# A two-layer hybrid backbone: small attention rows loaded first, output weights split during the convolution, and the value products of differential attention in parts

## The chip, the cores and the metric

The kernel runs on one core of one Trainium2 chip. The core has a matrix engine (PE, whose weight loads are listed apart as PEld), three engines for elementwise work (DVE, ACT, POOL), a queue engine (SP) that issues most DMAs, and 16 DMA engines that carry the transfers. The metric is the device time of one execution in microseconds. Three runs of the kernel before took 3598.65, 3591.5 and 3580.62 us, so their median is 3591.5 us.

## The reference

A backbone of two layers works on 1024 latent tokens and 256 context tokens, 1024 wide. Layer 0 mixes by gated linear attention and grouped-query attention, layer 1 by a Hyena convolution (512 channels) and differential attention (4 heads). Each mixer ends in one output projection, and a squared-ReLU MLP follows. The part that the change touches is the mixer of layer 1:

```python
def diff_attend(q, keys, vals, lam):
    ...
        s = jnp.einsum('bqhcd,bshcd->bhcqs', qblk, keys).astype(jnp.float32) * hd ** -0.5
        pr = jax.nn.softmax(s, axis=-1)
        a = (pr[:, :, 0] - lam * pr[:, :, 1]).astype(vals.dtype)
        return jnp.einsum('bhqs,bshv->bqhv', a, vals)
...
    y = out(diff_attend(q, jnp.concatenate([kc, k], axis=1), jnp.concatenate([vc, v], axis=1), lam))
...
    y = jnp.concatenate([y_c, y_d], axis=-1) @ w_out
```

Each head has two score matrices (c = 0, 1), whose softmaxes are subtracted with a learned factor lam before one product with 128-wide values. The result is normalised and scaled by a learned row `diff_g`. The Hyena half (`y_c`) is a projection, a short convolution, and two long convolutions by Fourier transform, each gated.

## The kernel before

**Numbers and tiles.** All matrices are float32. Most products are done as three faster products of parts: `split` (L92) copies a tile to a high part of type fp32r on ACT and subtracts it from the source on DVE (or POOL) for a low part, and `mm3` (L98) multiplies high by high, high by low and low by high into one PSUM bank. A PSUM bank holds 128 x 512 floats. The token axis is cut into NT = 10 tiles of 128 (two of context, eight of latent tokens).

**Order.** The program is written as generators. `weave` runs several of them side by side, each at a rate given in the code (a yield is one step), and `pipelined` keeps several items in flight. A scheduler then fixes the order of each engine's instructions when the program is built. Every engine runs its own list in that order, so an instruction that waits holds up all those behind it on its engine. SP issues DMAs in order too, and a DMA's issue can wait for a buffer.

**Layer 1, in time order** (times of the profiled execution):

- Up to about 2175 us the projection of layer 1 makes q, k and v of the differential attention. `in_proj1_v` (L1639) copies v to DRAM (`dv`) tile by tile, and q and k go to DRAM (`dq`, `dk`) from `qk_hi` and `qk_lo` (L1763), in parts.
- From there `diff_attn` (L2168) and `hyena` (L2503) are woven. The Hyena part begins with `hy_columns` (L1690): 12 blocks of 128 columns, 0 to 11; the weights of blocks 0 to 3 are loaded ahead, during the projection. A block loads its weights (`cb_raw`, two buffers, by SP), splits them (`cb_hi` on ACT, `cb_lo` on POOL, two buffers each), multiplies (`hc_ps`, L1683 to L1685), convolves (`hy_cv` on ACT and DVE), transposes (`cv_ps`) and stores (`hv<-hy_st`, issued by ACT, one buffer).
- `diff_attn` loads its keys and queries with `load` (L2175: `dkT`, two DMAs a head, and the buffer of the values `dvT`) and `load_q` (L2186: `dqT`, two DMAs for a group of 512 queries). Its work is 8 units, 4 heads by 2 query groups. A unit has 10 key steps. Each of the first eight key steps does one of the eight score rows of the next unit (`s_ps`, three pieces each, eviction by DVE maxima and ACT exponentials), then for its own unit `front` (four 128 x 128 transposes of probabilities into `pt_ps`, the one PSUM bank with the tag `tr`, and a copy `pt` by ACT) and `back` (one float32 product into `o_ps` with the values). 26 steps of the weave lie between the start of `diff_attn` and its first score.
- The load of the learned row, `df_gain` (L2263), of the lambda vectors, `df_lp`, and the small arithmetic on them (L2265 to L2276, on DVE and ACT) stand in the code after the first `load` and `load_q` and ahead of those 26 steps.
- After the last block and `diff_attn`, `hy_conv` (L1962) does the Fourier convolutions of the Hyena half: `forward`, `spectrum`, `backward`. The rest of the weave is `proj_half` (L1097), the attention half of the output projection (`ho_ps`, at rate 0.27). At the end `wo_rest` (L1089) loads and splits the four weight tiles for the Hyena half (`wo_raw`, `wo_hi` on ACT, `wo_lo` on POOL), `mlp_in` (L2339) reads the convolution's result back (`y_in<-hy`) and finishes the projection (`op_ps`), and the MLP follows.

## Time and profile before

| what | value |
|---|---|
| median of three runs | 3591.5 us (3580.62 to 3598.65) |
| the profiled execution's own time | 3587.32 us |
| its span in the profile | 3585.5 us |
| mean granted PE clock | 0.941 |
| PE busy in the span | 3158.2 us, 88% |
| DVE / ACT / POOL busy | 77% / 44% / 32% |
| all DMA traffic | 516.36 MB, mean 144 GB/s |

The profile shows one execution, and engines are busy side by side, so the shares don't add up to one. In the views, a row of a timeline has its start, its length, the engine, the source line, and what was written from what. In square brackets is the idle time ahead of it and the work that ended it. The stretch that the change touches begins at about 1970 us (the value projection) and ends at about 2890 us (the last output projections of layer 1). The rest of the span is the same code before and after.

### The profile page before, as it was taken

The page shows a single profiled execution, that of the slowest core. Times are in us where ns is not written, and L with a number is a line of the kernel's source. Part 1 is how long each engine was busy: PE and PEld are TensorE (multiplying, and loading weights), DVE is VectorE, ACT ScalarE, POOL GpSimd, SP SyncE. Part 2 cuts the span into 40 slices and gives each one's busy share as a digit, 9 for nine tenths or more (in the row PEclk, how much of TensorE's full clock was granted, in tenths as well). Part 3 has the DMA queues.
Part 4 walks back from the last instruction along what each step waited for, and adds up shares of the span by engine and source line. Part 5 has one row for each costly group of instructions (what it writes and reads, how often), then busy time and mean ns, then how long its engine had stood idle before and what let it go on. Part 6 is the DMA issues. An engine that isn't in the chain of part 4 may idle for free. (4 is left out here: it accounts for less than half of the span.)

```text
span 3585.5 us, 42317 instructions
## 1 busy us (share of the span) xinstructions
PE 3158.2 (88%) x13936; PEld 2451.6 (68%) x13936; DVE 2747.6 (77%) x4482; ACT 1560.3 (44%) x3186; POOL 1134.4 (32%) x796
## 2 busy tenths in 40 slices
PE   8888899799988999989998994988848689998996
PEld 4766677577766888767786773666636567887885
DVE  6788988787578666789888771767787589877989
ACT  5444666455563222343334631566632352225433
POOL 0254655323231222355554120100010212215654
PEclk9989999899999999999999997999979899999998
DMA  6543111667652333554543642222445635437442
GB/s 216 158 138 116 43 46 47 183 201 239 229 179 100 129 131 117 186 167 151 169 151 106 193 146 91 73 87 70 130 125 176 206 127 183 148 134 271 150 150 100
DMA packets 315961, 516.36 MB, mean 144 GB/s; under 512 B 39282, under 2 KB 138610, under 8 KB 315613
## 3 DMA queue, kind: packets, MB, share of 16 engines
q1 hardware_dynamic: 264708, 430.86, 36.9%
q10 hardware_dynamic: 41816, 49.24, 4.0%
q0 software_dynamic: 9216, 33.56, 3.4%
q8 instruction: 110, 1.80, 0.2%
q14 instruction: 111, 0.90, 0.1%
HBM read 364.21 MB, written 149.35 MB: 143 GB/s over the span
## 5 line engine op out<-in xcount | busy, mean ns | idle before, releaser
L95 POOL TENSOR_TENSOR dn_w_lo<-dn_b,dn_w_hi 128x512 fp32r<-128x512 f32 x224 | 358.8, 1626 | 317.3 <-ACT dn_w_hi L94 311.6
L1533 PE MATMUL dn_ps<-dn_w_hi,dn_h_hi 128*128 128x512 f32 x896 | 360.9, 403 | 40.5 <-DVE accy L1515 7.0
L1535 PE MATMUL dn_ps<-dn_w_hi,dn_h_lo 128*128 128x512 f32 x896 | 358.1, 400 | 13.4 <-DVE dn_h_lo L95 13.3
L1534 PE MATMUL dn_ps<-dn_w_lo,dn_h_hi 128*128 128x512 f32 x896 | 358.5, 400 | 9.4 <-POOL dn_w_lo L95 9.3
L95 POOL TENSOR_TENSOR w_lo<-up_w,w_hi 128x512 fp32r<-128x512 f32 x106 | 146.3, 1390 | 567.4 <-ACT w_hi L94 539.7
L94 ACT ACTIVATE dn_h_hi<-dn_h 128x512 fp32r<-128x512 f32 x224 | 139.1, 625 | 267.8 <-PE dn_ps L1534 172.3
L95 DVE TENSOR_TENSOR dn_h_lo<-dn_h,dn_h_hi 128x512 fp32r<-128x512 f32 x224 | 231.4, 1051 | 22.6 <-ACT dn_h_hi L94 20.3
L1533 PEld LDWEIGHTS dn_ps<-dn_w_hi,dn_h_hi 128*128 128x128 f32 x896 | 173.3, 193 | 87.7 <-DVE accz L1515 9.7
L765 POOL TENSOR_TENSOR gq_acc<-gq_acc,gq_p 128x512 f32<-128x512 f32 x128 | 183.8, 1436 | 88.5 <-ACT gq_p L754 85.1
L261 DVE SCALAR_TENSOR_TENSOR ada_acc<-w_ada,sc,ada_acc 128x512 f32<-128x512 f32 x224 | 194.2, 899 | 21.0 <-DMA w_ada<-in_w_ada 20.2
L1535 PEld LDWEIGHTS dn_ps<-dn_w_hi,dn_h_lo 128*128 128x128 f32 x896 | 173.4, 193 | 53.3 <-DVE dn_h_lo L95 16.7
L1534 PEld LDWEIGHTS dn_ps<-dn_w_lo,dn_h_hi 128*128 128x128 f32 x896 | 173.3, 193 | 48.9 <-POOL dn_w_lo L95 13.2
L95 DVE TENSOR_TENSOR gq_lo<-gq_p,gq_hi 128x512 fp32r<-128x512 f32 x168 | 176.2, 1061 | 19.7 <-ACT gq_hi L94 17.5
L94 ACT ACTIVATE s_hi<-up_w 128x512 fp32r<-128x512 f32 x128 | 79.1, 630 | 247.6 <-DVE up_w L1234 117.9
L647 DVE TENSOR_REDUCE sm_m<-s_ps 128x1 f32<-128x512 f32 (+1 forms) x192 | 110.9, 596 | 73.4 <-PE s_ps L637 72.4
L94 ACT ACTIVATE dn_w_hi<-dn_b 128x512 fp32r<-128x512 f32 x224 | 138.0, 621 | 52.3 <-DVE dn_b L1488 29.9
L1234 DVE TENSOR_TENSOR up_w<-up_w 128x512 f32<-128x512 f32 x128 | 93.6, 733 | 86.6 <-POOL w_lo L95 84.8
L104 PE MATMUL up_ps<-t_lo,s_hi 128*128 128x512 f32 x384 | 152.5, 397 | 2.0 <-DVE t_lo L95 2.0
L105 PE MATMUL up_ps<-t_hi,s_lo 128*128 128x512 f32 x384 | 151.6, 396 | 2.6 <-DVE s_lo L95 2.6
L1488 DVE TENSOR_TENSOR dn_b<-dn_b,dn_b 128x512 f32<-128x512 f32 x128 | 142.0, 1138 | 15.4 <-POOL dn_w_lo L95 15.3
L103 PE MATMUL up_ps<-t_hi,s_hi 128*128 128x512 f32 x384 | 151.5, 394 | 2.0 <-ACT t_hi L94 1.6
L94 ACT ACTIVATE w_hi<-up_w 128x512 fp32r<-128x512 f32 x106 | 64.8, 628 | 163.3 <-DMA up_w<-in_w_mlp_in 88.9
(513 smaller groups left out, 9306.1 us busy)
## 6 DMA issues: line engine op xcount, KB each, us to landing
w_ada<-in_w_ada SPq DMA_DIRECT2D x96, 512.0 KB
up_w<-in_w_mlp_in SPq DMA_DIRECT2D x32, 1024.0 KB
dn_b<-in_w_mlp_out SPq DMA_DIRECT2D x121, 256.0 KB
hy_m<-in_k_ff POOLq DMA_DIRECT2D x32, 512.0 KB, 5.5
x<-x_in SPq DMA_DIRECT2D x26, 512.0 KB
x_in<-x SPq DMA_DIRECT2D x26, 512.0 KB
cb_raw<-in_od_w_in SPq DMA_DIRECT2D x20, 512.0 KB
yh<-ho_o ACTq DMA_DIRECT2D x18, 512.0 KB
```

The source lines that it names most:

```text
L94: g.nc.scalar.activation(hi, src, ACTF.Copy)
L95: (g.nc.gpsimd if pool else g.nc.vector).tensor_tensor(lo, src, f(hi), op=ALU.subtract)
L103: nc.tensor.matmul(out, ah, bh, start=(i == 0), stop=False)
L104: nc.tensor.matmul(out, ah, bl, start=False, stop=False)
L105: nc.tensor.matmul(out, al, bh, start=False, stop=(i == n - 1))
L261: nc.vector.scalar_tensor_tensor(acc[:, s], w[:, k], sc, acc[:, s], op0=ALU.mult, op1=ALU.add)
L647: nc.vector.tensor_reduce(m[:, i:i + 1], s, axis=AX.X, op=ALU.max)
L765: nc.gpsimd.tensor_tensor(sums[u], sums[u], p, op=ALU.add)
L1488: nc.vector.tensor_tensor(d, x, y, op=ALU.subtract)
L1533: nc.tensor.matmul(ps, hh[:, sl], wh, start=first, stop=False)
L1534: nc.tensor.matmul(ps, hh[:, sl], wl, start=False, stop=False)
L1535: nc.tensor.matmul(ps, hl[:, sl], wh, start=False, stop=end)
```

## The change

The diff has five parts.

1. **Small rows first.** `df_gain` and `df_lp` are loaded at the start of `diff_attn`, the keys and queries of the first head at the third of the 26 steps, the first values and the second group of queries at the 15th. The arithmetic on the small rows comes after the 26 steps.
2. **Value products in parts.** The transposed probabilities are split into `pt_hi` (ACT, two buffers) and `pt_lo` (DVE, one buffer). The values are kept in DRAM and loaded as high and low parts, so a tile of values takes two stores where it took one, and a head's load is 1280 KB where it was 640 KB. Three fp32r products stand for one float32 product.
3. **Output weights in the convolution.** `wo_rest` is woven into the Hyena work at rate 0.06, the rate of `proj_half` falls from 0.27 to 0.2, and the raw weight tiles of both come from the pool of the parts that are kept, so that they share two buffers (layer 0 too).
4. **A buffer less.** The parts `hb` of the backward transform have two buffers where they had three.
5. **Sides.** The pools of layer 1's `mlp_in` and of the kept weights lie on the other side of the memory.

```diff
-def wo_part(g, w, kt, pool, by_pool):
-    raw = pool.tile([128, D], F32, name="wo_raw", bufs=2)
+def wo_part(g, w, kt, pool, by_pool, raws=None):
+    raw = (raws or pool).tile([128, D], F32, name="wo_raw", bufs=2)
     g.nc.sync.dma_start(out=raw, in_=w[kt * 128:(kt + 1) * 128, :])
...
-def proj_half(g, w, kts, tiles, y_of, pool, by_pool, mark=2):
+def proj_half(g, w, kts, tiles, y_of, pool, by_pool, mark=2, raws=None):
...
     for kt in kts:
-        wts.append(wo_part(g, w, kt, pool, by_pool))
+        wts.append(wo_part(g, w, kt, pool, by_pool, raws))
         yield mark
...
     nc = g.nc
-    g.dv = g.dram.tile([128, 4, NT, 128], F32, name="dv")
+    g.dv = g.dram.tile([128, 4, NT, 2, 128], F32, name="dv")
     def keep(t, ps):
-        v = pool.tile([128, 512], F32, name="dv", bufs=3)
-        nc.scalar.copy(v, ps)
-        nc.scalar.dma_start(out=g.dv[:, :, t, :], in_=v.rearrange("p (h e) -> p h e", h=4))
+        hl = [pool.tile([128, 512], FR, name=f"dv_{x}", bufs=2 - i) for i, x in enumerate(("hi", "lo"))]
+        split(g, *hl, ps)
+        for i, x in enumerate(hl):
+            nc.scalar.dma_start(out=g.dv[:, :, t, i, :], in_=f(x).rearrange("p (h e) -> p h e", h=4))
...
         z = load_z(1 + o, r)
-        bs = [parts(A[kt][r], "hb", 3) for kt in range(2)]
+        bs = [parts(A[kt][r], "hb", 2) for kt in range(2)]
         yield 1
...
             nc.sync.dma_start(out=f(k[:, c, :]), in_=g.dk[h][:, c * 64:c * 64 + 64, :])
-        v = kv.tile([128, NT, 128], F32, name="dvT", tag="dvT")
+        v = kv.tile([128, NT, 2, 128], FR, name="dvT", tag="dvT")
         heads[h] = k, v
...
         v = heads[h][1]
-        nc.sync.dma_start(out=v, in_=g.dv[:, h])
+        nc.sync.dma_start(out=f(v).rearrange("p t w e -> p (t w e)"), in_=g.dv[:, h].rearrange("p t w e -> p (t w e)"))
...
             nc.tensor.transpose(ps[:, i, :], a[i][k][:, o * 128:(o + 1) * 128], g.ident)
-        pt = pr.tile([128, 512], F32, name="pt", bufs=3)
-        nc.scalar.copy(pt, ps.rearrange("p a b -> p (a b)"))
-        return u, kt, pt
-
-    def back(u, kt, pt):
+        hi, lo = (pr.tile([128, 512], FR, name=f"pt_{x}", bufs=b) for x, b in (("hi", 2), ("lo", 1)))
+        split(g, hi, lo, ps.rearrange("p a b -> p (a b)"))
+        return u, kt, hi, lo
+
+    def back(u, kt, hi, lo):
         v = heads[u[0]][1]
...
             outs[u] = psa(g, [128, 512], name="o_ps", tag="o")
-        nc.tensor.matmul(outs[u], v[:, kt, :], pt, start=(kt == 0), stop=(kt == NT - 1))
+        nc.tensor.matmul(outs[u], v[:, kt, 0, :], hi, start=(kt == 0), stop=False)
+        nc.tensor.matmul(outs[u], v[:, kt, 1, :], hi, start=False, stop=False)
+        nc.tensor.matmul(outs[u], v[:, kt, 0, :], lo, start=False, stop=(kt == NT - 1))
         return u,
...
     units = [(h, qg) for h in range(4) for qg in range(2)]
-    load(0)
-    load_q(units[0])
     neg = tb.tile([128, 1], F32, name="neg")
...
     nc.sync.dma_start(out=gain, in_=g.i["od_diff_g"][0:1, :].partition_broadcast(128))
-    nc.vector.tensor_scalar(gain, gain, 1.0 - LAM_INIT, None, op0=ALU.mult)
     lp = tb.tile([128, 4, 64], F32, name="df_lp")
...
                       in_=g.i["od_lam"].rearrange("o a d -> o (a d)").partition_broadcast(128))
+    LATE = 1
+    for n in range(26):
+        if n == 2:
+            load(0)
+            load_q(units[0])
+        if n == 14:
+            load_v(0)
+            load_q(units[1])
+        yield
+    nc.vector.tensor_scalar(gain, gain, 1.0 - LAM_INIT, None, op0=ALU.mult)
     lm = tb.tile([128, 3], F32, name="df_lm")
...
     nlam = lm[:, 2:3]
-    load_v(0)
-    load_q(units[1])
-    LATE = 1
-    for _ in range(26):
-        yield
     for i in range(4):
...
-def mlp_in(g, layer, tiles, ctx, wo, y_of, x_src, x_dst):
+def mlp_in(g, layer, tiles, ctx, wo, y_of, x_src, x_dst, sides=("left", "right")):
+
...
     up_st, t_st, ps = ExitStack(), ExitStack(), ExitStack()
-    xp = up_st.enter_context(tc.tile_pool(name=f"x{layer}", bufs=1, reuse_waits="tile"))
-    up = Up(g, layer, *(up_st.enter_context(tc.tile_pool(name=f"{n}{layer}", bufs=1, reuse_waits="tile"))
+    xp = up_st.enter_context(tc.tile_pool(name=f"x{layer}", bufs=1, reuse_waits="tile", side=sides[0]))
+    up = Up(g, layer, *(up_st.enter_context(tc.tile_pool(name=f"{n}{layer}", bufs=1, reuse_waits="tile", side=sides[0]))
                         for n in ("up", "us")), ctx)
...
     early = up.early()
-    with tc.tile_pool(name=f"op{layer}", bufs=1, reuse_waits="tile") as pool:
+    with tc.tile_pool(name=f"op{layer}", bufs=1, reuse_waits="tile", side=sides[0]) as pool:
         def feat(t, h):
...
         wo.close()
-        up.t_first(x, xp, t_st.enter_context(tc.tile_pool(name=f"ta{layer}", bufs=1, reuse_waits="tile", side="right")))
+        up.t_first(x, xp, t_st.enter_context(tc.tile_pool(name=f"ta{layer}", bufs=1, reuse_waits="tile", side=sides[1])))
         heads = up.heads(pool)
...
         w = g.i["od_w_out"][0]
+        keep = pool_of(wo, "wo1", "left")
         with tc.tile_pool(name="ho1", bufs=1, reuse_waits="tile") as pool:
-            half = proj_half(g, w, range(4, KT), range(NC_T, NT), lambda t: y1d[t], pool, True, 0)
-            weave(hyena, (half, 0.27), rest=False)
-            weave(wo_rest(g, w, range(4), pool_of(wo, "wo1", "right"), True, 0), (half, 1.0))
+            half = proj_half(g, w, range(4, KT), range(NC_T, NT), lambda t: y1d[t], pool, True, 0, keep)
+            weave(hyena, (half, 0.2), (wo_rest(g, w, range(4), keep, True, 0), 0.06))
     mlp_in(g, 1, range(NC_T, NT), None, wo,
-           lambda t: g.hy[(t - NC_T) * 128:(t - NC_T + 1) * 128, :], x2, x3)
+           lambda t: g.hy[(t - NC_T) * 128:(t - NC_T + 1) * 128, :], x2, x3, ("right", "left"))
     with ExitStack() as st:
```

**On SP, around the first loads.** The first rows are SP's list before, from the first keys on (`dkT`, `dqT`, `dvT` are loads for the attention, `cb_raw` weights of a Hyena block, `dq<-qk` stores of queries):

```order
L2178 DMA dkT<-dk_18676 128x1x1280 x2
L1763 DMA dq_18675<-qk_hi 128x512
L1763 DMA dq_18675<-qk_lo 128x512
L2192 DMA dqT<-dq_18672 128x1x1024 x2
L2264 DMA df_gain<-in_od_diff_g 128x128
L2267 DMA df_lp<-in_od_lam 128x256
L2184 DMA dvT<-dv 128x1280
L2192 DMA dqT<-dq_18672 128x1x1024
L2178 DMA dkT<-dk_18677 128x1x1280
L1657 DMA cb_raw<-in_od_w_in 128x8x128
L2178 DMA dkT<-dk_18677 128x1x1280
```

The small rows now stand some 55 rows further up, among the loads of the projection before, and the rest of the list reads on without them. This is SP's list of the changed kernel from the same first keys on:

```order
L2179 DMA dkT<-dk_18706 128x1x1280 x2
L1764 DMA dq_18705<-qk_hi 128x512
L1764 DMA dq_18705<-qk_lo 128x512
L2193 DMA dqT<-dq_18702 128x1x1024 x2
L2185 DMA dvT<-dv 128x2560
L2193 DMA dqT<-dq_18702 128x1x1024
L2179 DMA dkT<-dk_18707 128x1x1280
L1658 DMA cb_raw<-in_od_w_in 128x8x128
L2179 DMA dkT<-dk_18707 128x1x1280
```

Apart from the two small loads and the size of the values, the order of the loads is the same, and the `cb_raw` in it is the weights of Hyena block 4 (counted from 0) in both.

**On PE, a key step of the attention.** Before, a step's transposes are followed by the product of the step ahead of it:

```order
L637 MATMUL s_ps<-dkT,dqT 128x256 x2
L637 MATMUL s_ps<-dkT,dqT 128x512 x4
L2227 MATMUL pt_ps<-ident,df_p_20292 128x128
L2227 MATMUL pt_ps<-ident,df_p_20369 128x128
L2227 MATMUL pt_ps<-ident,df_p_20467 128x128
L2227 MATMUL pt_ps<-ident,df_p_20543 128x128
L2236 MATMUL o_ps<-pt,dvT 128x512
L1683 MATMUL hc_ps<-ftx_hi,cb_hi 128x512
```

In the changed kernel the third product, the one with `pt_lo`, stands behind the next step's transposes, and the first two ahead of them:

```order
L2228 MATMUL pt_ps<-ident,df_p_20324 128x128
L2228 MATMUL pt_ps<-ident,df_p_20409 128x128
L2228 MATMUL pt_ps<-ident,df_p_20515 128x128
L2228 MATMUL pt_ps<-ident,df_p_20599 128x128
L2239 MATMUL o_ps<-pt_lo,dvT 128x512
L637 MATMUL s_ps<-dkT,dqT 128x256 x2
L637 MATMUL s_ps<-dkT,dqT 128x512 x4
L2237 MATMUL o_ps<-pt_hi,dvT 128x512
L2238 MATMUL o_ps<-pt_hi,dvT 128x512
```

The transposes write the bank that the subtraction for `pt_lo` has read, and the next `pt_lo` needs the buffer that the product behind the transposes reads.

**On POOL, the splits of the output weights.** Before, four of the eight `wo_lo` stand behind all loads of the transform's matrices (`hm`):

```order
L2009 DMA hm<-in_k_df 128x1024 x4
L2009 DMA hm<-in_k_di 128x1024 x8
L95 TENSOR_TENSOR wo_lo_24341<-wo_raw,wo_hi_24340 128x1024
L95 TENSOR_TENSOR wo_lo_24347<-wo_raw,wo_hi_24346 128x1024
L95 TENSOR_TENSOR wo_lo_24353<-wo_raw,wo_hi_24352 128x1024
L95 TENSOR_TENSOR wo_lo_24359<-wo_raw,wo_hi_24358 128x1024
L1072 TENSOR_TENSOR x_in<-x_in,y_h 128x1024
```

In the changed kernel the last of the eight stands ahead of most of those loads:

```order
L95 TENSOR_TENSOR wo_lo_24200<-wo_raw,wo_hi_24199 128x1024
L2010 DMA hm<-in_k_di 128x1024
L95 TENSOR_TENSOR wo_lo_24326<-wo_raw,wo_hi_24325 128x1024
L2010 DMA hm<-in_k_df 128x1024 x2
L2010 DMA hm<-in_k_di 128x1024 x2
L2010 DMA hm<-in_k_df 128x1024 x4
L2010 DMA hm<-in_k_di 128x1024 x8
L95 TENSOR_TENSOR w_lo<-up_w,w_hi 128x512 x4
```

What moved there is the split of the second four weight tiles, from after the convolution into it. On PE the attention half of the projection moves the other way: 36 more of its `ho_ps` products stand behind the last product of the convolution (`y_ps`).

More of the change, by code (lines that the diff above doesn't have):

```diff
@@ L2385, in mlp_in @@
         run(heads)
-    up.t_rest(t_st.enter_context(tc.tile_pool(name=f"tb{layer}", bufs=1, reuse_waits="tile", side="right")))
+    up.t_rest(t_st.enter_context(tc.tile_pool(name=f"tb{layer}", bufs=1, reuse_waits="tile", side=sides[1])))
     ps.close()
@@ L2433, in side0 @@
         with tc.tile_pool(name="ho0", bufs=1, reuse_waits="tile", side="right") as pool:
-            yield from proj_half(g, g.i["ev_w_out"][0], range(4, KT), range(NT), lambda t: yd[t][:, 512:], pool, False, 3)
+            yield from proj_half(g, g.i["ev_w_out"][0], range(4, KT), range(NT), lambda t: yd[t][:, 512:], pool, False, 3, keep)
             yield from wo_rest(g, g.i["ev_w_out"][0], range(4), keep, False, 3)
```

## The prediction

> **What bounds the kernel now.** I read the page first, for which engine is busy and where it isn't. Its row of the engines, and PE's busy tenths in 40 slices of 90 us:
>
> ```profile
> PE 3158.2 (88%) x13936; PEld 2451.6 (68%) x13936; DVE 2747.6 (77%) x4482; ACT 1560.3 (44%) x3186; POOL 1134.4 (32%) x796
> PE   8888899799988999989998994988848689998996
> ```
>
> PE bounds most of the span. In the part that the change touches there are three weak slices: a 4 (from 2151 us, the start of the attention), a 4 and a 6 (from 2600 and from 2779 us, the convolution). The list of waits from 2175 to 2300 us names the first hole, as engine, what waited, what it waited for, total, count, longest:
>
> ```profile
> DVE df_gain L2265 <- DMA df_gain<-in_od_diff_g: 47.2, 1, 47.2
> PE cv_ps L1705 <- DVE hy_cv L1727: 43.4, 2, 42.9
> ```
>
> DVE stands for 47.2 us at the first operation on the learned row. The short convolution of Hyena block 1 is queued behind it, and PE waits 42.9 us for that. What keeps a row of 64 KB away is seen in SP's timeline (start, length of the issue) and in the sums by window (busy time by engine, clock, DMA share, GB/s):
>
> ```profile
> 2160.48 1.18 SPq L2178 DMA_DIRECT2D dkT<-dk  x2
> 2174.73 11.99 SPq L2192 DMA_DIRECT2D dqT<-dq  x2
> 2186.81 10.26 SPq L2264 DMA_DIRECT2D df_gain<-in_od_diff_g  x1
> 2200.73 8.96 SPq L2178 DMA_DIRECT2D dkT<-dk  x1
> 2215.57 3.95 SPq L1657 DMA_DIRECT2D cb_raw<-in_od_w_in  x1
> core 0: us, PE busy (x) PEld busy (x) DVE busy (x) ACT busy (x) POOL busy (x), PEclk, DMA share, GB/s
> 2180.00:2197.00 17.00, 0.00 (x0) 0.00 (x0) 0.00 (x0) 0.00 (x0) 0.00 (x0) 0.51 0.13 53
> 2226.00:2237.00 11.00, 7.11 (x33) 5.34 (x31) 3.06 (x2) 3.30 (x4) 2.40 (x1) 1.00 0.13 52
> 2245.00:2252.00 7.00, 7.00 (x34) 5.79 (x33) 5.29 (x9) 2.80 (x4) 2.40 (x1) 1.00 0.13 52
> 2256.00:2276.00 20.00, 19.16 (x93) 15.57 (x93) 15.24 (x36) 13.52 (x35) 2.39 (x1) 1.00 0.20 58
> ```
>
> While nothing computes, 0.13 of 16 DMA engines, that is two, move 53 GB/s, and they are still at it at 2237 and at 2252. So the key and query loads run on one pair of lanes, one behind the other, and every other transfer has a share in the same two lanes and stands in line. A key load of 640 KB takes 12.4 us at that rate (0.655 MB by 53 GB/s), a query load of 512 KB 9.9 us.
>
> The Trainium skill's page "DMA: Bandwidth & Descriptors", section "Why a DMA increments its semaphore by 16 and not by 1", says that a DMA from these queues uses as many engines, at most 16, as divide the slowest dimension of both its patterns, and always the lowest-numbered ones; the query loads here begin with a dimension of 2. The share of 0.13 agrees.
>
> **Part 1, small rows first.** The rows move ahead of the key loads, so the 47.2 us at them go. What is late next? The weights of Hyena block 4 (`cb_raw` at 2215.57 in SP's rows) stand behind two key loads, three query loads and one more key load. Those are where they were, and the time at which the lanes take them is set by the same start, the issue at 2160. Before, I put the landing of these weights at about 2240 (the row falls behind the key load that ends at 2237). After, the values' load ahead of them is twice as long (640 KB more over 16 lanes, 1.5 us on each), and the stores of Hyena come earlier into the same line, so they land at about 2243.5. Their split comes next, and then PE's first product of block 4:
>
> ```profile
> 2244.89 1.06 ACT L94 ACTIVATE cb_hi<-cb_raw 128x1024 fp32r<-128x1024 f32 x1 [5.01 <-DMA hv<-hy_st]
> 2246.03 2.40 POOL L95 TENSOR_TENSOR cb_lo<-cb_raw,cb_hi 128x1024 fp32r<-128x1024 f32 x1 [16.56 <-ACT cb_hi L94]
> 2263.79 0.39 PE L1683 MATMUL hc_ps<-ftx_hi,cb_hi 128*128 128x512 f32 x1
> 2289.97 1.62 PE L637 MATMUL s_ps<-dkT,dqT 128*128 128x256 f32 x4 [2.85 <-DMA dqT<-dq]
> ```
>
> 2243.5 + 1.06 + 2.40 gives about 2247, against 2263.8 before: 17 us gained where 43 seemed to be had. Blocks 2 and 3 and the first scores run in the old hole, then PE stands for these weights. Further down the same lanes stands the second group of queries, for which PE waited at 2289.97 before. Behind one more key load, values and three weight loads I put it at 2280 to 2282, some 9 us earlier. So **−9**, with −5 and −17 as ends; −43 is the rival in which the lanes don't matter.
>
> **Part 2, value products.** The group of the products, and a piece of PE's timeline in which every start is visible:
>
> ```profile
> L2236 PE MATMUL o_ps<-pt,dvT 128*128 128x512 f32 x160 | 85.1, 615 | 0.0
> 2348.65 1.02 PE L2236 MATMUL o_ps<-pt,dvT 128*128 128x512 f32 x2
> 2349.11 0.80 PE L1683 MATMUL hc_ps<-ftx_hi,cb_hi 128*128 128x512 f32 x1
> 2349.75 0.40 PE L1684 MATMUL hc_ps<-ftx_lo,cb_hi 128*128 128x512 f32 x1
> 2349.98 0.40 PE L1685 MATMUL hc_ps<-ftx_hi,cb_lo 128*128 128x512 f32 x1
> 2350.22 0.39 PE L1683 MATMUL hc_ps<-ftx_hi,cb_hi 128*128 128x512 f32 x1
> ```
>
> Two records are one float32 product, so there are 80. From 2348.65 to 2349.75 PE does one of them and one fp32r product; fp32r products start 0.23 us apart. A float32 product thus takes 1.10 − 0.23 = 0.87 us, three fp32r ones 0.69, and PE saves 0.18 us a key step, 14 us in 80. For that DVE gets 80 subtractions. The nearest rows, one that reads a PSUM bank (the second from the page's groups reads the on-chip memory twice), and the dense stretch of the attention:
>
> ```profile
> L95 DVE TENSOR_TENSOR ho_lo<-ho_t,ho_hi x18: 672/684/693, 887.5 to 2767.7; 128x512 fp32r<-128x512 f32 x18
> L95 DVE TENSOR_TENSOR dn_h_lo<-dn_h,dn_h_hi 128x512 fp32r<-128x512 f32 x224 | 231.4, 1051 | 22.6 <-ACT dn_h_hi L94 20.3
> 2302.10:2352.40 50.30, 49.62 (x240) 36.22 (x239) 39.59 (x98) 36.52 (x99) 2.73 (x1) 1.00 0.21 67
> L2236 PE MATMUL o_ps<-pt,dvT 128*128 128x512 f32 x24 | 12.3, 593 | 0.0
> L2229 ACT COPY pt<-pt_ps 128x512 f32<-128x512 f32 x13 | 7.6, 587 | 5.6 <-PE pt_ps L2227 5.5
> ```
>
> The last two rows are of the same 50.3 us: 13 copies, so 13 key steps (24 records of products would be 12; some are missing, and with 12 both engines' steps grow by the same 8%). A step takes 50.30/13 = 3.87 us, PE nearly all of it, and DVE 39.59/13 = 3.05. After: PE 3.87 − 0.18 = 3.69, DVE 3.05 + 0.684 = 3.73. **DVE becomes the fuller one.** How full it can run, other stretches of this kernel show. They are from the convolution:
>
> ```profile
> 2580.00:2613.50 33.50, 26.82 (x106) 17.44 (x105) 28.60 (x51) 15.28 (x36) 2.11 (x4) 0.90 0.37 110
> 2613.50:2660.00 46.50, 10.10 (x30) 5.42 (x28) 44.34 (x65) 6.04 (x14) 0.00 (x0) 0.60 0.33 95
> 2740.00:2790.00 50.00, 29.16 (x111) 21.51 (x109) 49.90 (x59) 9.70 (x14) 0.00 (x0) 0.77 0.30 109
> ```
>
> DVE is busy 95% in the second and 99.8% in the third, but 85% in the first, where it hands to PE and back. At 95% a step takes 3.73/0.954 = 3.91 us, 0.04 more than now, times 80 is +3. At 99.8% it is 3.74, −10; at 85% 4.37, +40. With subtractions of 1.05 us at 95% it is (3.05 + 1.05)/0.954 = 4.30, +34. I take **+3**, the middle row, since the scheduler has other DVE work to put between, and keep −10 and +40.
>
> On which of the two durations holds, the page "SBUF — State Buffer" of the Trainium skill, section "Who interferes with whom", says that a DVE instruction with at most one input in SBUF doesn't contend with GpSimd (POOL). The subtraction reads one operand from PSUM, so by that rule it stays at 0.684 also beside POOL's work, as the row of `ho_lo` has it, and the term is +3, not +34.
>
> The last units reach into the first spectrum stage (2580 to 2613.5, the row above, and the DVE-bound stage behind it). There PE's saving is worth nothing and DVE is full. Some 20 of the 80 steps' subtractions fall there or push work there: 20 x 0.684 = 14 us of DVE, of which DVE's 4.9 idle us of that first row and a part of the stages' start absorb half: **+7** (0 to +14). The values' second part in the projection adds ten subtractions (7 us) to a DVE that is busy 56 of 80 us, and ten stores:
>
> ```profile
> 1980.00:2060.00 80.00, 76.81 (x356) 62.28 (x356) 56.23 (x112) 49.66 (x104) 13.80 (x7) 0.98 0.70 205
> ```
>
> PE covers them: **+1** (0 to +5; all ten subtractions bare would be +7, but DVE is idle for 24).
>
> **Part 3, output weights.** The middle of the convolution, where PE is the bound, and the end, where it isn't; then what was waited for there:
>
> ```profile
> 2660.00:2740.00 80.00, 72.49 (x309) 58.34 (x310) 46.16 (x55) 26.76 (x37) 21.10 (x20) 0.94 0.64 199
> 2816.00:2837.00 21.00, 11.05 (x43) 7.90 (x44) 1.38 (x2) 5.43 (x6) 9.40 (x4) 0.84 0.88 308
> ACT wo_hi L94 <- DMA wo_raw<-in_od_w_out: 18.1, 4, 13.2
> PE tr_ps L1155 <- DMA y_in<-hy: 7.9, 1, 7.9
> L95 POOL TENSOR_TENSOR wo_lo<-wo_raw,wo_hi x8: 2347/2366/5165, 2663.3 to 2831.8; 128x1024 fp32r<-128x1024 f32 x8
> L95 DVE TENSOR_TENSOR wo_lo<-wo_raw,wo_hi x8: 1206/1225/1577, 882.3 to 922.4; 128x1024 fp32r<-128x1024 f32 x8
> 2669.67 2.21 DVE L95 TENSOR_TENSOR hblo<-ht,hbhi 128x1024 fp32r<-128x1024 f32 x1 [0.40 <-ACT hbhi L94]
> ```
>
> 36 attention products leave the middle: 36 x 0.23 = −8 there, as PE is 91% busy. Four more weights enter its ACT and POOL lists and delay the transform's operands: I take half of that saving back, +4. A DVE subtraction of 128 x 1024 takes 1.23 us in the row of `wo_lo` on DVE, and 2.21 in the last row, beside a POOL split. Four moved splits cost up to 1 us each: **+3** (0 to +4). So −4 and +3. At the end PE idles 10 of 21 us. The 36 products (8 us) fill that, the chain of raw weights, `wo_hi` and `wo_lo` is gone, but the read-back `y_in` stays, behind two loads of 1 MB each: 2 MB at 308 GB/s are 7 us, where 1 MB stood before. I take **−5**, with −10 and +3.
>
> **Part 4, a buffer less.** Two `hb` of 128 x 1024 are all that one backward step uses; the third let the next step's first part begin early. Nothing shows its worth; the nearest row is that a split takes 1.06 on ACT and 1.2 to 2.2 on DVE, a few of them bare: **+2** (0 to +5). Part 5 and the shared raw buffers of layer 0 I take as nothing: the splits there are hidden by PE, and uncovered they would cost one split (2.4 us).
>
> **Sum.** −9 + 3 + 7 + 1 − 4 + 3 − 5 + 2 = −2, against the profiled execution's own 3587.3 (span 3585.5): 3585. That execution lies 4 us below the median of 3591.5, so against the median this is −6, no change within half a per cent, 18 us either way (about what a measurement of this kernel can tell from no change): faster is below 3573.5, slower above 3609.5.
>
> **The rivals.**
>
> - *The hole closes in full.* If block 4's weights come earlier than I work out, because its row's lanes take turns rather than stand in line, PE runs on. Then −43 stands for −9, the rest as above: 3551. For it: DMA moves only 53 GB/s in the hole. Against it: two lanes are busy without a break from 2180 to 2252.
> - *DVE holds the attention up, and the kernel is slower.* The transposes' bank is freed only by `pt_lo`; in the changed order the next transposes wait for it, and the third product stands behind them. A step then has in series four transposes (about 0.5), a copy of about 0.6, a subtraction of 0.68, and each handover queues behind other work. If that leaves DVE 85% busy, as in the first convolution row, the price is +40 in place of +3: 3622. The kernel is slower by more than half a per cent once DVE is busy under 89% there (3.73/0.885 = 4.21 us a step, +28). For it: one bank, one buffer, and three engines in turn. Against it: those 1.8 us in series leave 1.9 of the step for queueing.
> - *The first part does nothing.* If the second group of queries lands no earlier than at 2289.97, since all of the same bytes are on its two lanes and SP issues three weight loads ahead of it, the −9 goes: 3594.
>
> **How the numbers follow.** The forecast has 0.44, of which 0.08 lies below 3573.5 and 0.04 above 3609.5 by its own bounds. The full closing has 0.22 (0.21 faster, 0.01 same), the slower attention 0.24 (0.21 slower, 0.03 same), nothing from the first part 0.10 (same). Faster 0.29, same 0.46, slower 0.25. The range leaves a tenth out at each side: down to 3553, near the middle of the first rival, up to 3618, short of the second's by four. The forecast's own range is 3569 to 3603.
>
> **What would show it.** Right: no wait at `df_gain`; PE at work from 2175 and then standing for `cb_raw` until about 2247; a first product of block 4 there, and the query wait at 2280 to 2282; `pt_lo` near 0.69 us; key steps of 3.7 to 4.0 us where they took 3.87; the wait for `wo_raw` at the end gone. Wrong: block 4 at 2225 or earlier (first rival), a step above 4.2 us with PE waiting for `pt_lo` (second), a query wait unmoved (third), or a new wait in the convolution that costs more than 10 us.

## The result, and the profile after

| | before | changed |
|---|---|---|
| median | 3593.68 us (3580.62 to 3598.65, 4 runs) | 3626.95 us (3614.7 to 3627.57, 4 runs) |
| span of the profiled execution | 3585.5 us | 3624.5 us |

The ratio is 1.0085, with a 95% interval of 1.0068 to 1.0102: the change makes the kernel about 30 us slower. The page's rows of the engines and of PE in 40 slices, after:

```profile
PE 3179.7 (88%) x14016; PEld 2474.4 (68%) x14016; DVE 2807.5 (77%) x4572; ACT 1560.8 (43%) x3186; POOL 1137.2 (31%) x796
PE   8978899799979999889998995888857789998997
```

PE has 21 us more work and DVE 60. The 4 at the start of the attention has become a 5, and the convolution reads 5, 7, 7 from the 30th slice on, where it read 4, 8, 6 (a slice is now 90.6 us). The list of waits from 2100 to 2350 us shows that the learned row is no longer in it, and what is there in its place:

```profile
POOL cb_lo L95 <- ACT cb_hi L94: 146.5, 6, 38.3
ACT cb_hi L94 <- DMA cb_raw<-in_od_w_in: 25.8, 2, 21.1
ACT cb_hi L94 <- DMA dqT<-dq: 23.9, 1, 23.9
PE cv_ps L1706 <- DVE hy_cv L1728: 21.0, 2, 20.5
PE s_ps L637 <- ACT hy_u L1717: 11.2, 2, 10.8
```

The two waits of ACT, in its timeline, and what PE does at their end:

```profile
2180.26 0.59 ACT L1707 COPY hy_st<-cv_ps 128x512 f32<-128x512 f32 x1 [0.77 <-PE cv_ps L1706]
2204.28 0.38 ACTq L1709 DMA_DIRECT2D hv<-hy_st  x1
2204.71 1.06 ACT L94 ACTIVATE cb_hi<-cb_raw 128x1024 fp32r<-128x1024 f32 x1 [23.86 <-DMA dqT<-dq]
2244.93 1.06 ACT L94 ACTIVATE cb_hi<-cb_raw 128x1024 fp32r<-128x1024 f32 x1 [21.07 <-DMA cb_raw<-in_od_w_in]
2246.52 1.22 PE L637 MATMUL s_ps<-dkT,dqT 128*128 128x512 f32 x2 [10.80 <-ACT hy_u L1717]
2294.72 1.62 PE L637 MATMUL s_ps<-dkT,dqT 128*128 128x256 f32 x4 [3.31 <-DMA dqT<-dq]
2384.52 1.19 PE L637 MATMUL s_ps<-dkT,dqT 128*128 128x256 f32 x3 [11.93 <-DMA dqT<-dq]
```

ACT has finished the first Hyena store's data at 2180.85 and issues the store at 2204.28: the issue itself waits, until a query load lands. The packed trace tells why: ahead of the store ACT waits for semaphore 99, which the first query load (issued by SP at 2177.55) raises as it lands, at 2204.20, and which the store raises in its turn. Load and store have no data in common; they share a semaphore. The split of block 3 and the copies for block 2 stand behind this wait. Then the split of block 4 waits for its weights until 2244.93, as forecast (2243.5), and the scores wait for a copy that stands behind that split. They go on at 2246.5, where they began before (2246.24), and the second queries come at 2294.7, not at 2280. Block 4's first product comes at 2263.17; the forecast was 2247, and before it came at 2263.79. So the hole is broken into pieces: PE is busy 17.6 us of the first 43 and 13.6 of the next 28, where it was 0.2 and 22.8:

```profile
2175.00:2218.00 43.00, 17.56 (x77) 13.54 (x75) 6.06 (x4) 5.12 (x7) 3.03 (x2) 0.72 0.29 99
2218.00:2246.00 28.00, 13.59 (x50) 10.94 (x50) 1.12 (x2) 2.24 (x4) 0.00 (x0) 0.68 0.34 104
```

Most of the loss comes later. The wait for queries at the first head's end (2384.52 above) is 11.9 us where it was 8.8. The subtraction has the duration that was forecast; its row in the view by tile (shortest, median and longest in ns, first and last start):

```profile
L95 DVE TENSOR_TENSOR pt_lo<-pt_ps,pt_hi x80: 667/683/692, 2300.8 to 2664.7; 128x512 fp32r<-128x512 f32 x80
```

The last ten key steps lie in the first spectrum stage. DVE's timeline there has the subtractions in line behind the transform's operations:

```profile
2645.54 0.68 DVE L95 TENSOR_TENSOR pt_lo<-pt_ps,pt_hi 128x512 fp32r<-128x512 f32 x1
2646.14 1.21 DVE L1990 TENSOR_TENSOR hw<-hw,hk 128x1024 f32<-128x1024 f32 x1
2647.27 1.22 DVE L1987 TENSOR_TENSOR hw<-hw 128x1024 f32<-128x1024 f32 x1
2648.41 0.68 DVE L1987 TENSOR_TENSOR ht<-ht,hw 128x512 f32<-128x512 f32 x1
2649.01 0.68 DVE L1984 TENSOR_TENSOR ht<-ht,hw 128x512 f32<-128x512 f32 x1
2649.61 0.68 DVE L95 TENSOR_TENSOR pt_lo<-pt_ps,pt_hi 128x512 fp32r<-128x512 f32 x1
```

DVE is busy 40.9 of the 41 us from 2623 to 2664. Before, the last ten steps came in the 15.6 us from 2599.8 to 2615.3; now they take from 2623.2 to 2663.7, 4.5 us a step (starts of the copies out of the transposes' bank). PE's transposes wait for the subtraction in front of them little in the steps up to 2543 us (first line, from 2300) and much in the last ones (second line, to 2664):

```profile
PE pt_ps L2228 <- DVE pt_lo L95: 2.7, 4, 1.5
PE pt_ps L2228 <- DVE pt_lo L95: 13.3, 9, 2.6
```

### The profile page after: what moved, and what is told of

Same layout as the page of the kernel before. It is cut to its first block, busy times and chain, and to the rows that moved or that the text cites. A ratio compares the mean times of both kernels' runs of the same rounds, so it can differ in the third digit from the quotient of the medians.

```text
span 3624.5 us, 42687 instructions
## 1 busy us (share of the span) xinstructions
PE 3179.7 (88%) x14016; PEld 2474.4 (68%) x14016; DVE 2807.5 (77%) x4572; ACT 1560.8 (43%) x3186; POOL 1137.2 (31%) x796
## 4 chain that ended last, share of the span: by engine, by line
PE 27%; DVE 11%; DMA 5%; issue 4%; SPq 2%; ACT 2%; POOL 1%; ACTq 0%; DVEq 0%; POOLq 0%
PE dn_ps L1535 3%; PE dn_ps L1533 3%; PE dn_ps L1534 3%; PE up_ps L105 2%; PE up_ps L103 2%; PE up_ps L104 2%; PE s_ps L637 1%; DMA dqT<-dq 1%; DMA cb_raw<-in_od_w_in 1%; PE hc_ps L1684 1%; SPq L2179 1%; PE hc_ps L1685 1%; PE hc_ps L1686 1%; DVE dn_h_lo L95 1%; DMA w_ada<-in_w_ada 1%
## 5 line engine op out<-in xcount | busy, mean ns | idle before, releaser
L1533 PE MATMUL dn_ps<-dn_w_hi,dn_h_hi 128*128 128x512 f32 x896 | 361.4, 403 | 43.3 <-ACT dn_w_hi L94 11.9
L1533 PEld LDWEIGHTS dn_ps<-dn_w_hi,dn_h_hi 128*128 128x128 f32 x896 | 173.6, 194 | 90.0 <-ACT dn_w_hi L94 13.2
L261 DVE SCALAR_TENSOR_TENSOR ada_acc<-w_ada,sc,ada_acc 128x512 f32<-128x512 f32 x224 | 202.7, 937 | 10.0 <-DMA w_ada<-in_w_ada 9.1
L1534 PEld LDWEIGHTS dn_ps<-dn_w_lo,dn_h_hi 128*128 128x128 f32 x896 | 173.8, 194 | 47.0 <-POOL dn_w_lo L95 11.5
L637 PE MATMUL s_ps<-dkT,dqT 128*128 128x512 f32 (+1 forms) x384 | 106.6, 382 | 44.6 <-DMA dqT<-dq 23.0
```

The costliest lines, as they stand in the source:

```text
L261: nc.vector.scalar_tensor_tensor(acc[:, s], w[:, k], sc, acc[:, s], op0=ALU.mult, op1=ALU.add)
L637: g.nc.tensor.matmul(o[:, b:e], ql, kr[:, k0 + b:k0 + e], start=(w == 0), stop=(w == 1))
L1533: nc.tensor.matmul(ps, hh[:, sl], wh, start=first, stop=False)
L1534: nc.tensor.matmul(ps, hh[:, sl], wl, start=False, stop=False)
```

## The experiments

Each is compared with the kernel before, in the same session. A ratio of 1.0010 is 3.6 us.

### One part at a time

**e1.** Part 1 alone: the diff's hunks in `diff_attn` from `units` to `nlam`.

> The kernel before with part 1 alone (small rows first, arithmetic on them after the 26 steps). Theory: the wait at the learned row (47.2 us) goes, but ACT then stands some 20 to 24 us at the issue of the first Hyena store, until a query load lands at about 2201, and the split of block 4 still waits for its weights until about 2242 to 2245; the first key step's copy starts within 5 us of the 2294.4 of before, and the time is -5 to +5 us against before. Rival (my forecast of this part): blocks 2 and 3 run at once, the first key step is 9 us earlier, the time -9. Rival (full closing): -35 to -43.

Measured: 1.0009 (0.9995 to 1.0022). Nothing changes, and not even the wait goes:

```profile
DVE df_gain L2275 <- DMA df_gain<-in_od_diff_g: 47.0, 1, 47.0
PE cv_ps L1705 <- DVE hy_cv L1727: 43.1, 2, 42.6
```

The time lies in the theory's range, but not for its reason: the wait that all three expectations took away stays. The scheduler leaves the load where it was, behind the query loads (2188.25 in SP's timeline, 2186.81 before).

**e2.** Parts 2 and 4: the hunks of `in_proj1_v`, `load`, `load_v`, `front`, `back`, and `"hb", 2`.

> The kernel before with parts 2 and 4 (value products in parts, two buffers for the parts of the backward transform, without which the values do not fit). Theory: the key steps of the first six units keep their length within 0.05 us, and the loss sits where the last two units share DVE with the first spectrum stage; the copy of the last unit's output ends some 30 us later than the 2617 of before, and the time is +18 to +28 us. Rival: the loss of the whole change comes from the start of the attention or from the output weights, and this one is 0 to +8.

Measured: 1.0082 (1.0065 to 1.0098), +29 us: the whole loss. And here the wait at the learned row is gone, without part 1, with ACT's 23.9 us and the 21.0 at the weights in its place, as in the changed kernel. SP issues the load at 2058.1 here and at 2055.0 in the changed kernel, 2186.8 before. In the trace of before, that load waits for a semaphore of DVE as well as for a DMA's; in the changed kernel it waits for a DMA's alone. That points to the memory that the tile gets when the values grow, which was not tried apart; it is not its place in the code. The theory had the loss a little too small and its place wrong: the units don't keep their length (the table below), and the copy of the last unit's output ends at 2667.9, 50 us later than before and not 30.

**e3.** Parts 3 and 5 alone.

> The kernel before with parts 3 and 5 (output weights split inside the convolution, attention half at rate 0.2). Theory: the end loses its wait for raw weights, the middle gains nothing, -8 to 0 us. Rival: the splits on POOL beside DVE's subtractions of 128 x 1024 and the loads of the transform's matrices behind them on POOL cost more than the end gains: +5 to +12.

Measured: 1.0009 (0.9999 to 1.0020). Neither the gain nor the loss is shown: the interval is -0.4 to +7 us. The wait for raw weights at the end is gone, as forecast, but PE's wait for the read-back `y_in` stays (7.3 us, before 7.9), and the last output product comes 0.3 us later.

**e4.** Part 4 alone: `"hb", 3` becomes `"hb", 2`.

> The kernel before with part 4 alone (two buffers in place of three for the parts of the backward transform). Theory: 0 to +3 us. Rival: the third buffer let the next step's high part be made while the products still read the other two, and without it PE waits in every backward step: +8 to +15.

Measured: 1.0008 (0.9998 to 1.0017), +3 us, as the theory had it.

### What in the value products costs

**e5.** e2 with the float32 product, on tiles and transfers of the new size:

```diff
-        split(g, *hl, ps)
+        v = pool.tile([128, 512], F32, name="dv", bufs=3)
+        nc.scalar.copy(v, ps)
+        for i in range(2):
+            nc.scalar.dma_start(out=g.dv[:, :, t, i, :], in_=v.rearrange("p (h e) -> p h e", h=4))
...
-        split(g, hi, lo, ps.rearrange("p a b -> p (a b)"))
+        pt = pr.tile([128, 512], F32, name="pt", bufs=3)
+        nc.scalar.copy(pt, ps.rearrange("p a b -> p (a b)"))
...
+        nc.tensor.matmul(outs[u], v[:, kt, 0, :], pt, start=(kt == 0), stop=(kt == NT - 1))
```

> The kernel of e2 with one float32 product a key step again: no split of the probabilities, but the values are still stored twice and loaded at 1280 KB a head, in the same tiles (both stored copies are the float32 value, and the second is not used). It takes DVE's subtractions and the three products away and keeps the memory layout and the transfers. Theory: the loss of the whole change has two places, about 8 to 12 us at the start of the attention (the wait at the learned row is gone, but ACT stands at the issue of the first Hyena store, and block 4 waits for its weights), and the rest in DVE's subtractions; so +5 to +12 us against before here. Rival: all of the loss is DVE's, and this one is -9 to +2.

Measured: 1.0018 (1.0008 to 1.0028), +6.5 us, the theory's range. Its start has the same two waits of ACT (23.8 and 20.8 us), so closing the wait at the learned row this way gains nothing.

**e6.** e2 without `pt_lo` and without its product, and with three buffers for `pt_hi`.

> The kernel of e2 without the low part of the probabilities: no subtraction on DVE, and two fp32r products a key step (the low part is left out of the computation). Theory: the last units no longer crowd the first spectrum stage, the last key step is within 5 us of where e5 has it or earlier, and PE saves 0.41 us a step where it is the bound, so -15 to 0 us against before. Rival: the loss sits in the start, the transfers and the two-part values, not in the subtraction: +15 to +25.

Measured: 1.0010 (0.9999 to 1.0020), +4 us. The 25 us between e6 and e2 go with the low part, but the two cheaper products earn little: the +4 lies outside both expectations, near the theory's. The trace shows where the saving goes. From the first to the 56th key step PE waits for queries for 32.1 us, where it waited for 16.0 before:

```profile
PE s_ps L637 <- DMA dqT<-dq: 32.1, 2, 18.4
PE s_ps L637 <- DMA dqT<-dq: 16.0, 2, 8.8
```

PE reaches these waits sooner, and the loads don't land sooner.

**e7.** e2 with `nc.gpsimd.dma_start` for the store of `hv`.

> The kernel of e2 with Hyena's stores issued by POOL and not by ACT. Theory: ACT's 23.9 us at the issue of the first store go, blocks 2 and 3 and the first scores run some 20 us earlier, but block 4 still waits for its weights until 2243 to 2250 and the second group of queries lands no earlier, so the first key step moves by less than 5 us and the time is +22 to +29 us against before. Rival: the wait at the issue is what eats the gain, and the time is +5 to +14.

Measured: 1.0080 (1.0063 to 1.0097), as e2. The waits from 2165 to 2300 us:

```profile
ACT cb_hi L94 <- DMA cb_raw<-in_od_w_in: 56.1, 2, 51.5
PE s_ps L637 <- ACT hy_u L1717: 29.1, 2, 28.7
```

ACT's wait at the issue is gone, and the wait behind it, for block 4's weights, has grown to 51.5 us. That is the wait that the forecast named; the store only came first.

**e9.** e6 with a third product, of the high parts once more; the low part of the probabilities is left out.

> The kernel of e6 with a third product a key step, of the high parts once more (wrong on the values, right in cost): the changed kernel's PE work without DVE's subtraction and without the wait for it. Theory: the third product costs PE 0.23 us in 80 steps, at most 18 us, less where PE waits anyway, so 0 to +10 us against before; the subtraction is what costs the rest of e2's +29. Rival: the third product is the cost, +20 to +29.

Measured: 1.0019 (1.0008 to 1.0030), +7 us, so the theory. The third product costs some 3 us over e6, though the two intervals overlap.

**e10.** e9 with a DVE operation in every key step whose result nobody reads, and with two buffers for `pt_hi` in place of three:

```diff
+        lo = pr.tile([128, 512], FR, name="pt_lo")
+        nc.vector.tensor_tensor(lo[:, 0:320], f(hi)[:, 0:320], f(hi)[:, 192:512], op=ALU.subtract)
```

> The kernel of e9 with a subtraction of 320 columns of the high part on DVE in every key step, about 0.68 us, whose result nobody reads: DVE's work as in e2, but the transposes' bank is freed by ACT and PE waits for nothing of DVE's. Theory (DVE is full where the last two units meet the first spectrum stage): 15 to 25 us more than e9, near e2's +29. Rival (the handover: one bank and one buffer through three engines): within 5 us of e9, and e2's loss is the wait of PE's transposes for DVE.

Measured: 1.0032 (1.0021 to 1.0043), +11.5 us, so 5 more than e9, which is the rival's range. But the operation is shorter than meant, 0.483 us where the subtraction takes 0.683 (first line), and something does wait for it: ACT's copy into a buffer that DVE has yet to read (second line, 2534 to 2646 us):

```profile
L2232 DVE TENSOR_TENSOR pt_lo<-pt_hi x80: 464/483/494, 2302.3 to 2651.1; 128x320 fp32r<-128x320 f32 x80
ACT pt_hi L2230 <- DVE pt_lo L2232: 16.9, 6, 4.5
```

So e10 tests 0.7 of DVE's fill, and not without any wait. Scaled up, the fill would cost some 7 us over e9 (an estimate, 4.7 x 0.683/0.483). The 18 us between e10 and e2 hold the rest of the fill, PE's need of the result, and the order that the scheduler builds from it.

**e13, e14, e15.** The kernel before with the split and three products, but with the high part of the values only. One low buffer; two; and the bank freed by ACT:

```diff
+        pt = pr.tile([128, 512], F32, name="pt")
+        nc.scalar.copy(pt, ps.rearrange("p a b -> p (a b)"))
+        nc.scalar.copy(hi, pt)
+        nc.vector.tensor_tensor(lo, pt, f(hi), op=ALU.subtract)
```

> The kernel before with the probabilities split as in the change (two buffers for the high part, one for the low) and three fp32r products, but only the high part of the values, which is used in all three (the low part of the values is left out): stores, loads and layout stay as before, and memory for one more buffer is free. It is the base for e14 and e15. Theory (the handover through one bank and one buffer costs what e2 has over e10): +18 to +28 against before, although the start is that of before. Rival: the doubled loads of values were needed for the loss, +8 or less.

> The kernel of e13 with two buffers for the low part. Theory A (the bank is the limit: PE's transposes wait until DVE has read it): within 4 us of e13. Theory B (the buffer is the limit: DVE cannot write the low part until PE has done the product behind the next transposes): 8 to 18 us below e13.

> The kernel of e13 with the transposes' bank freed by ACT: ACT copies it to a float32 tile (one buffer), makes the high part from that tile, and DVE subtracts from that tile; one copy of about 0.6 us a step more on ACT, and DVE's subtraction reads two tiles in memory (about 1.05 us). Theory A (bank): 5 to 15 us below e13 in spite of the longer operations. Theory B (buffer): 0 to 12 us above e13.

Measured: 1.0035 (1.0022 to 1.0048), 1.0031 (1.0020 to 1.0043) and 1.0032 (1.0021 to 1.0044). All three are one: neither a second buffer nor a bank that ACT frees gains anything by itself, so theory B fails in e14 and theory A in e15. Each run takes one of the two limits away and leaves the other; both together were not tried. The traces show the wait moving. From the 56th step to the last, in e13 and then in e15:

```profile
PE pt_ps L2227 <- DVE pt_lo L95: 13.1, 9, 2.6
PE o_ps L2241 <- DVE pt_lo L2232: 17.2, 10, 3.3
```

With the bank freed early, PE waits for the low part at the product that reads it. And +12.5 us is less than the theory had for e13, more than the rival. The longer operation that was expected in e15 did not come: with both operands in the on-chip memory the subtraction takes 0.683 us in the median too. The longest, 2.47 us, began while POOL was in a split.

**e16.** e13 with two buffers `hb`.

> The kernel of e13 (probabilities split, three products, high part of the values only, loads and layout as before) with two buffers for the parts of the backward transform, as e2 has them. Theory (the attention that ends later meets the convolution, and the missing third buffer costs 8 to 12 us there, where e13 gained 6): +20 to +26 against before, so that e2's +29 is this plus the start. Rival: the buffer costs its 3 us of e4 here too, +13 to +17, and what is left of e2 comes from the doubled loads.

Measured: 1.0053 (1.0035 to 1.0071), +19 us: between the two. The buffer that cost 3 us alone costs 6.5 here, though the intervals of e13 and e16 overlap. Where each kernel stands against before, in us, at five points of the profiled execution (start of the first and of the 56th copy out of the transposes' bank; first `hblo`; last `y_ps`; last `op_ps`):

| | first key step | 56th | first `hblo` | last `y_ps` | last `op_ps` |
|---|---|---|---|---|---|
| before | 2294.35 | 2524.26 | 2651.9 | 2813.6 | 2889.2 |
| e3, weights inside | -0.1 | -0.3 | +6.4 | -0.3 | +0.3 |
| e4, two `hb` | +0.4 | +0.5 | -1.8 | +7.0 | +1.1 |
| e5, layout and transfers | +4.1 | +4.7 | +4.8 | +10.7 | +6.1 |
| e9, three products | +7.6 | +10.7 | +10.3 | +16.7 | +12.3 |
| e10, and DVE's 0.48 us | +7.3 | +10.5 | +15.5 | +21.9 | +14.7 |
| e13, old layout | -2.9 | +10.2 | +16.5 | +10.5 | +10.7 |
| e16, and two `hb` | -1.1 | +11.7 | +21.9 | +29.2 | +22.7 |
| e2 | +7.6 | +20.3 | +30.7 | +35.6 | +30.7 |
| changed kernel | +5.8 | +19.0 | +35.8 | +33.8 | +35.6 |

From the first to the 56th step, e2, e13, e16 and the changed kernel lose 12.7 to 13.2 us, e9 and e10 3.1 and 3.2, and e5 0.6. So DVE's operation adds nothing there as long as nobody reads its result (e10 less e9), and some 10 us come with the subtraction whose result PE needs.

From there to `hblo`, e9 loses nothing, e10 5, e13 6, e2 and e16 10. So in this stage DVE's fill costs by itself. What e2 and e16 have over e13 is a wait of 3.7 us that e13 has not, for a matrix of the transform:

```profile
PE fa_ps L103 <- DMA hm<-in_k_df: 3.7, 1, 3.7
```

The changed kernel has it too (4.0 us) and loses 17 up to `hblo`. But e3 loses 7 there by part 3 alone and has it back at the last `y_ps`, so this is the place of that instruction and not time.

In the convolution, e13 gains 6, and the kernels with two `hb` lose 5 to 9 and have most of it back at the last `op_ps` (the changed kernel, with the weights' splits there, goes the other way). e2 and e16 differ by the start, 8.7 us, and go nearly alike from there. So e2's 31 us at the last `op_ps` are 8 at the start, 13 in the units and 10 in the first spectrum stage; the buffer takes away what e13 gains behind it.

### The lanes

**e8 and e11.** e2, and the kernel before, with each key and query load in two halves:

```diff
-            nc.sync.dma_start(out=f(k[:, c, :]), in_=g.dk[h][:, c * 64:c * 64 + 64, :])
+            for x in range(2):
+                nc.sync.dma_start(out=f(k[x * 64:x * 64 + 64, c, :]), in_=g.dk[h][x, c * 64:c * 64 + 64, :])
...
-            nc.sync.dma_start(out=f(q).rearrange("p w t -> p (w t)"), in_=src.unsqueeze(0).to_broadcast([2, 64, 1024]))
+            for x in range(2):
+                nc.sync.dma_start(out=f(q[x * 64:x * 64 + 64]).rearrange("p w t -> p (w t)"), in_=src)
```

> The kernel of e2 with each key and query load in two halves of 64 partitions, which has a first dimension of 64 in both patterns. Theory: the loads then use all 16 lanes and take 2 to 4 us each; the hole at the start closes to under 10 us, the waits for queries in the units (some 23 us in e2) go, and the time is 40 to 65 us below e2, so -10 to -35 against before. Rival: DVE with its subtractions sets the units' pace, and only the hole's 20 to 30 us come back: 0 to +8 against before. Rival: the halves are no faster than the whole, and nothing changes.

> The kernel before with each key and query load in two halves of 64 partitions, nothing of the change. Theory: the hole and the waits for queries go as in e8, without DVE's subtractions: 15 to 30 us below e8's 3528, so -75 to -90 against before. Rival: with the loads out of the way PE is the bound in the units, the cheaper products earn their 14 us, and this one is at e8's time or up to 10 us above it.

Measured: e8 0.9827 (0.9813 to 0.9842), median 3528.1 us, 63 below before and 90 below e2, more than the theory's 40 to 65; e11 0.9792 (0.9772 to 0.9813), median 3515.6 us, 75 us less than before. The sums of e11 by window, after the last column of which stand GB/s:

```profile
2175.00:2190.00 15.00, 14.09 (x68) 11.07 (x66) 5.33 (x10) 5.91 (x9) 2.40 (x1) 1.00 1.01 262
2190.00:2218.00 28.00, 27.91 (x133) 22.68 (x132) 16.83 (x40) 16.35 (x39) 4.80 (x2) 1.00 0.38 106
```

All 16 lanes move 262 GB/s where two moved 53, and PE is busy 42.0 of the 43 us that were the hole. The rival in e11 falls: also with the loads out of the way the value products in parts lose, 12.5 us between the medians (e11 to e8), a little less than the theory's 15 to 30. No wait for queries is left in the units of either. From the first to the 56th key step e11 takes 210.8 us and e8 218.8, so 8 us of the loss in the units don't need such a wait.

**e12.** e11 with parts 1, 3 and 5.

> The kernel of e11 with parts 1 and 3 to 5 without 4 (small rows first in the code, output weights inside the convolution; float32 value products, three buffers). Theory: e11's time within 5 us, since the scheduler places the small rows by the memory that they get, and the output weights earned nothing in e3. Rival: with the start closed the weights' place counts: 5 to 12 us below e11.

Measured: 0.9818 (0.9791 to 0.9844), median 3522.9 us. With the intervals overlapping, no gain over e11 is shown. e11 has the lowest median of all.

## Why the prediction was wrong

Forecast was 3585 with 3553 to 3618; it is 3627, slower, beyond the range and on the side of the second rival (3622).

- **Part 1, -9: wrong.** The step that failed is "Blocks 2 and 3 and the first scores run in the old hole". The weights of block 4 came when I said. But the -17 compared their split with a PE row 19 us behind it: the same split stood at 2244.89 before, and block 3's products and the first scores lay between it and the product at 2263.79. In the changed kernel block 3 does begin 15 us earlier (2230.0 for 2244.9), but the scores among its products wait for ACT, which stands at that split, so block 4 begins 0.6 us earlier and not 17. And block 3 itself stands some 20 us behind ACT's other wait, at the issue of a store (PE idles from 2190 to 2211). That one I had not seen at all: I followed the queues of SP and PE, not ACT's. The first key step is 5.8 us later, not 9 earlier. And the code lines that I credited do nothing (e1); the layout of part 2 moved the load. "The first part does nothing" is what e1 shows of the code; the move of the load, which came from part 2, costs +6.5 with its transfers and the two `hb` (e5).
- **The key steps, +3: mis-sized, +13.** The subtraction's length was right: 0.683 us, at most 0.692, and 0.68 in the three that ran beside a POOL split of 2.4 us (the Trainium skill's page "SBUF — State Buffer", section "Who interferes with whom", agrees). The 1.05 us kept beside it were misread as the price of two operands in the on-chip memory: e15 has 0.683 for that. The step that failed is that a key step takes the time of its fuller engine, 3.73 us of DVE at 95%, with PE's saving of 0.18 us behind it. PE's saving is worth nothing while the queries come when they come: with three products and no subtraction (e9) the 56 steps get 3 us longer, and the waits for queries in them grow from 16.0 to 25.9 us. DVE's fill costs nothing in these steps either, as far as e10 tests it. The subtraction that PE needs costs 10 more.

  The rival, a DVE that holds the attention up, had the engine right, and its 3622 is near by luck. It asked for 4.37 us a step throughout. The units lose 0.24 a step, and a good part of the rest is DVE's fill in the first spectrum stage and the start. Its wait for the bank is there, 2.7 us in the units and 13.3 in the last steps, but with the bank freed early the wait goes to the product (e15).

  How the 10 us in the units come about stays open: PE idles for 29.8 us there in the changed kernel and for 30.6 in e9, so longer waits are not where the 10 us lie. Some 2 us are ten more of Hyena's products between the two steps (316 for 306 in e9); the rest are products that start further apart. One piece can be read from the changed order, not from a run: the last key steps of a unit pair now come behind PE's wait for queries and not ahead of it. In the changed kernel the 20th copy is at 2389.2, after the wait that ends at 2384.5; before, it was at 2363.7, ahead of the wait that ended at 2376.4. So less work covers that wait. It is not the whole: e15, whose 20th copy (2374.4) still lies ahead of that wait (to 2381.9), loses 11 us in the units as well, and e8, without such waits, 8 against e11.
- **The first spectrum stage, +7: mis-sized.** It is +10 in e2, of which 3.7 are the wait for the matrix that no term had; e13, without that wait, has 6. The +17 in the changed kernel (36 less 19) holds the 7 that e3 shows to be no loss.
- **The output weights, -6: not borne out.** e3 shows +3, with 0 within its interval; the read-back `y_in`, which I had left standing, holds the end. The two `hb`, +2: +3 alone (e4), and 6.5 between e13 and e16, where the attention runs later into the convolution, both near the noise: a term that I added as if it stood alone.
- **The projection, +1:** the first key load is issued 2.6 us later (2163.06 for 2160.48 in SP's timeline), within its 0 to +5.
- **The lanes: right.** That the key and query loads run on two lanes in one line was the reading that bore out best. The rule of the Trainium skill's page "DMA: Bandwidth & Descriptors", section "Why a DMA increments its semaphore by 16 and not by 1", agrees: halves with a first dimension of 64 fill all lanes (1.01 in e11's window).

## What to carry to other kernels

When a wait is taken away, follow every in-order queue to its next wait, the engine that only issues a store included (it can wait for a semaphore that an unrelated load holds), and compare the same instruction before and after. A saving on an engine that then waits for a load is no saving. A product split into parts moves work to a second engine. Where that engine is full, its fill is the price (the spectrum stage); where it isn't, the price came only with the first engine's need of the result (the units). Look at the share of the DMA engines in the hole before moving loads about: here one extra loop, which let the loads use all 16 lanes, was worth 75 us, and the rearrangement around them nothing.

## What was not expected of the hardware

After a hole, PE's products start further apart for a while. In the changed kernel the fp32r products after the hole, the first, two of the last slow ones, and two at the usual pace:

```profile
2211.48 0.78 PE L1684 MATMUL hc_ps<-ftx_hi,cb_hi 128*128 128x512 f32 x1
2226.88 0.63 PE L1685 MATMUL hc_ps<-ftx_lo,cb_hi 128*128 128x512 f32 x1
2227.31 0.63 PE L1686 MATMUL hc_ps<-ftx_hi,cb_lo 128*128 128x512 f32 x1
2228.64 0.40 PE L1684 MATMUL hc_ps<-ftx_hi,cb_hi 128*128 128x512 f32 x1
2228.88 0.40 PE L1685 MATMUL hc_ps<-ftx_lo,cb_hi 128*128 128x512 f32 x1
```

They are 0.43 us apart and then 0.24; from the end of the second piece of the hole at 2222.1 it takes 5.6 us until the pace changes. The Trainium skill's page "TensorE: Matmul & The Clock Gate", section "What's actually happening", tells of half the clock after an idle window and of about 3.4 us of activity until it is released; the half agrees, and the time here is longer. In the kernel before it is 3.4 us, from the end of the hole at 2218.1 to about 2221.5. The granted clock in the two windows of the broken hole is 0.72 and 0.68, where PE was busy 17.6 and 13.6 us; before, it was 0.56 in the one hole of 43 us and 0.88 after it. The slow start comes back with each piece: at 2211, 2222 and 2247 in the changed kernel, and at 2218 and 2238 before. How many of the 6 us at the start this makes was not measured apart.
